# Gated linear attention: one product of 128 columns for two chunks' scores, and all low parts of the input projection's weights on VectorE

## The chip, the cores and the metric

The kernel runs on one core of a Trainium2 chip. The metric is the device time of one execution in microseconds (us). The engines are named as in the profile: PE (TensorE, matrix products), DVE (VectorE), ACT (ScalarE), POOL (GpSimd) and SP (SyncE, which issues most DMAs). Each engine has its own row of instructions, in the order in which the program issued them; an instruction waits on semaphores until what it reads is there.

## The reference, cut to what matters

One layer of a decoder for 512 prompt tokens and 8 x 4 sample tokens (544 in all), all in float32:

```python
proj = rmsnorm(x) @ w_in                 # 2048 -> 6160 columns: GLA q, k, v, gate, low-rank gate; attention q, k, v
S_t = diag(a_t) S_{t-1} + k_t^T v_t      # gated linear attention (GLA), 4 heads, key width 128, value width 256
o_t = q_t S_t
# dilated attention, 8 heads of 128: windows (128,1), (512,4), (2048,16), combined by their log-sum-exp;
# for the prompt within its 512 tokens, for the sample against a cache of 2048 rows
x = x + concat(gla_part, att_part) @ w_out
y = x + square(relu(rmsnorm(x) @ w_up)) @ w_down
```

What matters here are the scores of GLA within a chunk of 128 tokens, `A[t,s] = sum_k q[t,k] k[s,k] exp(b[t,k] - b[s,k])` for `s <= t`, with `b` the running sum of the log gates.

## The kernel before, in words

**Products in two parts.** A float32 product is made of three products of a faster format (fp32r, shown as `R32` in the code). A weight tile `raw` is rounded by ACT to its high part `wh`, and the difference `raw - wh` becomes the low part `wl`; activations are split in the same way. Each product is then wh·xh + wh·xl + wl·xh.

**The input projection** goes over 48 blocks of 128 columns (`order`), each in two slots `i` (one for each half of the 2048 rows), so that slots 0 to 95 are the projection and from slot 96 on comes w_out. Each slot has two quarters `q` of 128x512 weights. For a half slot PE does 16 products of 128x272 with `wh`, then the background work due, then 8 with `wl` (`slot_main`, L1023). `load_to` keeps three raw tiles ahead; `prep_to` calls `split_q` (L233) for the next quarter, which emits the ACT cast (`wh`) and the subtraction (`wl`), with three `wh` and three `wl` buffers. The subtraction is on POOL for slots 4 to 95 (`POOL_M` = 15: all quarters; 180 tiles in all), on DVE for the others (64 tiles). The later stages, w_up and w_down, have code of their own, in which DVE makes all low parts.

**Background work** is put between these products by `bg` (L288). It runs two lists of generators: `sgens`, the sample's attention (its step is four DVE operations on a tile `kv` of 128x640 from the cache), put in as long as the planner's clock for DVE is behind that for PE, and `gens`: the prompt's attention by heads (`att_prompt`, L437), the four GLA heads (`gla`, L685), and a norm (`att_norm`). The planner's clocks come from `Engine.cost` (L98), a price for each instruction. These prices decide where background work is put, and so the order of every row. All engine calls go through one helper, so that nearly all instructions carry its line, L95.

**An attention head** runs: scores on PE, exponent shift and maximum (custom DVE operations with the tile `st`), exp on ACT, a reciprocal on DVE, the scaling by it on ACT (out `b`, in `b,st`), transposes on PE (in `cst,b`, the identity is in `cst`), and products with v.

**A GLA head** makes the scores by levels `[64, 32, 16, 8, 4, 2, 1]`: at level w the chunk of 128 tokens is cut into blocks of 2w; queries of each block's second half (`u=1`) meet keys of its first half (`u=0`). `lev_a` (L738) takes differences of `b` against the block's middle (two DVE operations of 128x256: one for each `u`) and the exp on ACT; `lev_b` (L748) multiplies with q and k (two of 128x256) into one tile E; `lev_c` (L755) makes four products of 128x64 (one for each of the four chunks, E as the stationary operand, its `u=1` columns moving) and one COPY_PREDICATED of 128x256 into `AT` under a mask `msk`. Levels go in pairs: a step on DVE is `lev_a` of one pair, the copies of the pair before, and `lev_b`.

Of the kernel before, what the change touches and what calls it, by code (L numbers as in the profile page):

```python
# [9 lines left out]
AF = mybir.ActivationFunctionType  # L10
# [24 lines left out]
SG_C = 60  # L35
NG_A = 1
NG_G = 2
POOL_M = 15
TH_G = 2000
TH_S = 1000  # L40
LAG = 10000
# [9 lines left out]
S_FIX = 27  # L51
NUB = 4
UD = 2
POOL_SUB = 96
LEVELS = [64, 32, 16, 8, 4, 2, 1]

GQ, GK, GV, GG, GLR, AQ, AK, AV = 0, 512, 1024, 2048, 3072, 3088, 4112, 5136
# [23 lines left out]
class Engine:  # L81
# [16 lines left out]
    def cost(self, name, a, k):  # L98
        n = width(a[1] if name == "tensor_reduce" else a[0])
        if self.key == "P":  # L100
            if name == "transpose":
                return 109
            if a[1].dtype == R32:
                return 116
            return 1.68 * n if n >= 128 else 426
        if self.key == "S":
            return 100 + 0.83 * n
        if self.key == "G":
            return 120 + 2.25 * n
        if name == "tensor_copy" or name == "memset":  # L110
            return 60 + 0.7 * n
        if name == "reciprocal":
            return 60 + 6.3 * n
        return 65 + 1.07 * n + (65 if k.get("accum_out") is not None else 0)
# [8 lines left out]
def _body(ctx, nc, tc, A):  # L123
# [22 lines left out]
    def alloc(dt=F32):  # L146
        cnt[0] += 1
        n = f"b{cnt[0]}"
        for free, p, tag, bufs in tiers:
            if free[0]:  # L150
                free[0] -= 1
                t = p.tile([128, NTOK], dt, name=n, tag=tag, bufs=bufs)
                home[id(t)] = (t, free)
                return t
        raise SystemExit(f"no slots at {slot[0]} {unit_no}")
# [75 lines left out]
        spl[key] = clk[eng.key]  # L231

    def split_q(i, q):  # L233
        split_w((i, q), raws[i][:, 4 * q:4 * q + 4, :], G if 4 <= i < POOL_SUB and POOL_M >> (i % 2 * 2 + q) & 1 else V)

    def load_to(n):
        while loaded[0] < n:
# [447 lines left out]
    def gla(h):  # L685
# [49 lines left out]
        S.activation(xs[:, :128], xs[:, :128], AF.Exp)  # L735
        E = {}

        def lev_a(i):  # L738
            w = LEVELS[i]
            e = E[i] = alloc()  # L740
            ev = e[:, :SEQ].rearrange("p (n u w) -> p n u w", u=2, w=w)
            bw = bb[:, :SEQ].rearrange("p (n u w) -> p n u w", u=2, w=w)
            ref = bw[:, :, 0, w - 1:w].to_broadcast([128, SEQ // (2 * w), w])
            V.tensor_sub(ev[:, :, 1, :], bw[:, :, 1, :], ref)
            V.tensor_sub(ev[:, :, 0, :], ref, bw[:, :, 0, :])
            S.activation(e[:, :SEQ], e[:, :SEQ], AF.Exp)

        def lev_b(i):  # L748
            w = LEVELS[i]
            ev = E[i][:, :SEQ].rearrange("p (n u w) -> p n u w", u=2, w=w)  # L750
            for u, s in ((1, q), (0, k)):
                sv = s[:, :SEQ].rearrange("p (n u w) -> p n u w", u=2, w=w)
                V.tensor_mul(ev[:, :, u, :], ev[:, :, u, :], sv[:, :, u, :])

        def lev_c(i):  # L755
            b = balloc()
            w = LEVELS[i] if i < 7 else 1
            for c in range(4):
                cs = slice(c * 128, (c + 1) * 128)
                if i < 7:  # L760
                    P.matmul(b[:, c * 64:(c + 1) * 64], E[i][:, cs],
                             E[i][:, cs].rearrange("p (n u w) -> p n u w", u=2, w=w)[:, :, 1, :], start=True, stop=True)
                else:
                    P.matmul(b[:, cs], k[:, cs], q[:, cs], start=True, stop=True)
            if i < 7:
                n = 64 // w
                V.copy_predicated(AT.rearrange("p c (n u w) -> p c n u w", u=2, w=w)[:, :, :, 1, :],
                                  msk[:, i, :].rearrange("p (n u w) -> p n u w", u=2, w=w)[:, None, :, 1, :]
                                  .to_broadcast([128, 4, n, w]),
                                  b[:, :256].rearrange("p (c n w) -> p c n w", c=4, w=w))  # L770
                rel(E.pop(i))
            else:
                V.copy_predicated(AT, msk[:, i:i + 1, :].to_broadcast([128, 4, 128]),
                                  b.rearrange("p (c t) -> p c t", c=4))
            brel(b)
# [82 lines left out]
                     start=b < 4, stop=b >= 4)  # L858
        for j in range(2):
            P.transpose(b2[:32, j * 128:(j + 1) * 128], vv[j][:, SEQ:], ident)  # L860
        os_ = [alloc(), alloc()]
        tm = xs[:, 384:]
        av = b0[:, :128].rearrange("p (d b i) -> p d b i", d=4, i=4)
# [38 lines left out]
        for j in range(2):  # L902
            while len(bfree) < 1:
                yield "wait"
            b0 = balloc()
            for c in range(4):
                cs = slice(c * 128, (c + 1) * 128)
                P.matmul(b0[:, cs], vtok[:, c, j * 128:(j + 1) * 128], AT[:, c, :], start=True, stop=c == 0)
                if c:
                    P.matmul(b0[:, cs], ST[:, c, j * 128:(j + 1) * 128], qe[:, cs], start=False, stop=True)  # L910
            S.activation(os_[j][:, :SEQ], b0, AF.Copy)
            brel(b0)
            yield
        rel(qe)
        turn[0] += 1
        sq = [alloc(), alloc()]
        for j in range(2):
# [161 lines left out]
    def drain(cond, lst):  # L1079
        n = 0  # L1080
        while not cond():
            slot[0] += 1
            begin()
            clk["P"] = max(clk["P"], clk["V"], clk["S"])
            bg(2)
            n += 1
            assert n < 1000
        if DEBUG:
            print("drained", n)
# [716 lines left out]
def shape_consts():  # L1806
    f = np.float32
    cst = np.zeros((128, 546), f)
    cst[:, :128] = np.eye(128)
    s = np.arange(128)  # L1810
    cst[:, 128:256] = (s[:, None] <= s[None, :]) / 16.0
    t = np.arange(32)
    cst[:32, 256:288] = ((t[:, None] // 4 == t[None, :] // 4) & (t[:, None] <= t[None, :])) / 16.0
    bm = (np.arange(8)[:, None] == t[None, :] // 4)
    cst[:, 288:544] = bm.reshape(1, 256)
    for g in range(2):
        cst[:, 544 + g] = [SLOPES[4 * g + p // 32] for p in range(128)]
    msk = np.zeros((128, 8, 128), f)
    a, b = s[:, None], s[None, :]
    for i, w in enumerate(LEVELS):  # L1820
        msk[:, i] = (a // (2 * w) == b // (2 * w)) & (a % (2 * w) < w) & (b % (2 * w) >= w)
    msk[:, 7] = np.eye(128)

    def mult(d):
        return ((d >= 0) & (d <= 128)).astype(f) + ((d >= 0) & (d % 4 == 0) & (d <= 512)) + \
            ((d >= 0) & (d % 16 == 0) & (d <= 2048))
    d = np.arange(128)[:, None] + 384 - np.arange(512)[None, :]
    c = mult(d).astype(f)
    dc = np.stack([np.where(c > 0, -d, -1e30), np.log(np.maximum(c, 1))]).astype(f)
    i = np.arange(128) % 4  # L1830
    dist = sample_dist(i)
    c = mult(dist).astype(f)
    dcs = np.stack([np.where(c > 0, -dist, -1e30), np.log(np.maximum(c, 1))]).astype(f)
    return cst, msk, dc, dcs
# [83 lines left out]
```

## Time and profile before

| | before |
|---|---|
| median of 3 runs | 2343.21 us (2341.41 to 2343.31) |
| the profiled execution, device time | 2339.07 us |
| its span in the trace | 2337.3 us |
| mean granted PE clock | 0.996 |
| PE busy | 2289.7 us (98%) |
| DVE busy | 1993.4 us (85%) |
| ACT busy | 1114.4 us (48%) |
| POOL busy | 418.7 us (18%) |

The projection with its background work lies from about 100 to 840 us of the span; the steps of w_out, w_up and w_down follow. A row of the timeline gives the start and the length in us, the engine, the code line, the operation, its output tile and inputs, shapes, and the number of instructions run together; in square brackets stands how long the engine was idle before, and what released it. A row of the groups gives the busy time in us, the mean ns of one, and the idle time before. A row of the windows gives, for a stretch of the span, its length, the busy us of PE, PE's weight loads, DVE, ACT and POOL (with the number of instructions), the granted PE clock (1.00 is full), the DMA share and GB/s.

### The profile page before, as it was taken

To read this page: it belongs to the slowest core of one execution; us is meant where nothing else is said; L and a number is where in the kernel's file an instruction comes from. 1 tells how busy PE (TensorE), PEld (TensorE's weight loads), DVE (VectorE), ACT (ScalarE), POOL (GpSimd) and SP (SyncE) were. 2 spreads that over 40 slices of the span, in tenths; PEclk is the share of its full clock that TensorE was granted. 3 is DMA by queue.
4 is the path that set the end of the run, shared out by engine and by line. 5 is a ranking of instruction groups with operands and counts; after the bars stand their busy time and mean duration, and the time that the engine had idled before them with its cause. 6 is when DMAs were issued, how large, how long until landed. Compare 5 with 4: busy or idle time off the path is not lost.

```text
span 2337.3 us, 47617 instructions
## 1 busy us (share of the span) xinstructions
PE 2289.7 (98%) x18064; PEld 2262.0 (97%) x18064; DVE 1993.4 (85%) x4096; ACT 1114.4 (48%) x2097; POOL 418.7 (18%) x377
## 2 busy tenths in 40 slices
PE   8999999999999999899999999999999999999997
PEld 8999999999999998899999999998999999999997
DVE  6998987898887988888888888887788888888995
ACT  5333333333344235566666666665544444444465
POOL 3544553333444553000000000000000000000000
PEclk9999999999999999999999999999999999999999
DMA  6776865554725975355665556656754654664564
GB/s 239 253 265 246 291 224 206 175 175 154 248 79 166 332 243 200 113 184 195 197 208 183 185 192 208 195 185 249 272 174 161 228 200 153 223 211 156 170 215 151
DMA packets 168193, 473.46 MB, mean 203 GB/s; under 512 B 20091, under 2 KB 29307, under 8 KB 167964
## 3 DMA queue, kind: packets, MB, share of 16 engines
q1 hardware_dynamic: 157340, 439.67, 55.5%
q0 software_dynamic: 9472, 29.63, 3.9%
q8 instruction: 142, 2.33, 0.4%
q10 hardware_dynamic: 1152, 1.11, 0.1%
q14 instruction: 87, 0.71, 0.1%
HBM read 393.07 MB, written 77.27 MB: 201 GB/s over the span
## 4 chain that ended last, share of the span: by engine, by line
PE 85%; DVE 9%; issue 2%; ACT 2%; DMA 1%; SPq 0%; POOL 0%; DVEq 0%; ACTq 0%; POOLq 0%
PE bank L95 85%; DVE b L95 7%; ACT b L95 1%; DVE wl L95 1%; DMA b<-hs 0%; DVE wlP L95 0%; DVE AT L95 0%; ACT wh L95 0%; DMA kv<-kcg 0%; DVE kv L95 0%; DMA b<-vs 0%; DMA b<-xT 0%; DMA b<-wglr 0%; POOL b L95 0%; ACT L932 0%
## 5 line engine op out<-in xcount | busy, mean ns | idle before, releaser
L95 PE MATMUL bank<-b,whP 128*128 128x272 f32 x6720 | 984.5, 289 | 12.7 <-DVE b L95 4.0
L95 PEld LDWEIGHTS bank<-b,whP 128*128 128x128 f32 x6720 | 897.3, 189 | 17.0 <-ACT whP L95 5.7
L95 PE MATMUL bank<-b,wlP 128*128 128x272 f32 x3360 | 558.4, 288 | 1.1 <-DVE wlP L95 1.1
L95 PE MATMUL bank<-b,wh 128*128 128x272 f32 x3904 | 532.1, 289 | 6.1 <-ACT wh L95 5.9
L95 PEld LDWEIGHTS bank<-b,wh 128*128 128x128 f32 x3904 | 505.9, 189 | 8.5 <-ACT wh L95 8.3
L95 PEld LDWEIGHTS bank<-b,wlP 128*128 128x128 f32 x3360 | 474.4, 189 | 2.3 <-DVE wlP L95 2.3
L95 ACT ACTIVATE b<-b 128x544 fp32r<-128x544 f32 (+7 forms) x485 | 274.4, 571 | 246.6 <-DVE b L95 213.9
L95 ACT ACTIVATE whP<-b 128x512 fp32r<-128x512 f32 x480 | 300.8, 627 | 180.8 <-PE bank L95 127.9
L95 DVE TENSOR_TENSOR wlP<-b,whP 128x512 fp32r<-128x512 f32 x480 | 329.6, 688 | 29.8 <-PE bank L95 23.9
L95 POOL TENSOR_TENSOR wl<-raw,wh 128x512 fp32r<-128x512 f32 x180 | 271.0, 1511 | 384.0 <-ACT wh L95 313.0
L95 DVE TENSOR_TENSOR b<-b,b 128x272 f32<-128x272 f32 (+8 forms) x531 | 286.6, 555 | 50.5 <-ACT b L95 44.5
L95 POOL TENSOR_TENSOR b<-b,b 128x544 f32<-128x544 f32 (+2 forms) x41 | 58.3, 1425 | 1465.9 <-ACT b L95 1465.3
L95 PE MATMUL bank<-b,wl 128*128 128x272 f32 x1952 | 297.7, 295 | 0.0
L95 PEld LDWEIGHTS bank<-b,wl 128*128 128x128 f32 x1952 | 262.0, 189 | 5.9 <-issue 3.9
L95 ACT ACTIVATE wh<-raw 128x512 fp32r<-128x512 f32 x244 | 150.5, 623 | 182.0 <-PE bank L95 162.0
L95 ACT ACTIVATE b<-bank 128x272 f32<-128x272 f32 (+5 forms) x243 | 96.8, 409 | 280.2 <-PE bank L95 262.2
L95 DVE TENSOR_TENSOR b<-b,bank 128x272 f32<-128x272 f32 x388 | 167.4, 434 | 62.6 <-PE bank L95 62.2
L95 DVE TENSOR_TENSOR wlP<-mraw,whP 128x512 fp32r<-128x512 f32 x206 | 142.2, 690 | 41.0 <-ACT whP L95 40.6
L95 ACT ACTIVATE whP<-mraw 128x512 fp32r<-128x512 f32 x206 | 127.7, 626 | 89.2 <-PE bank L95 83.6
L95 DVE SCALAR_TENSOR_TENSOR kv<-kv,b 128x320 f32<-128x320 f32 x256 | 160.7, 687 | 1.6 <-DMA kv<-vcg 1.6
L95 PE MATMUL bank<-b,b 128*128 128x272 f32 (+5 forms) x968 | 143.7, 305 | 6.3 <-ACT b L95 6.3
L95 PEld LDWEIGHTS bank<-b,b 128*128 128x128 f32 (+2 forms) x968 | 119.8, 181 | 12.2 <-ACT b L95 6.4
(89 smaller groups left out, 1799.5 us busy)
## 6 DMA issues: line engine op xcount, KB each, us to landing
hs<-b SPq DMA_DIRECT2D x196, 272.0 KB, 6.0
b<-hs SPq DMA_DIRECT2D x196, 272.0 KB, 5.1
raw<-win SPq DMA_DIRECT2D x90, 512.0 KB, 4.8
mraw<-wdn SPq DMA_DIRECT2D x82, 512.0 KB, 3.9
kv<-kcg SPq DMA_DIRECT2D x64, 640.0 KB, 5.0
kv<-vcg SPq DMA_DIRECT2D x64, 640.0 KB, 4.9
mraw<-wup SPq DMA_DIRECT2D x74, 512.0 KB, 4.3
raw<-wdn SPq DMA_DIRECT2D x62, 512.0 KB, 3.8
```

The source lines that it names most:

```text
L95: return f(*a, **k)
```

## The change

**Scores.** For each level and each pair of chunks (2c, 2c+1) there is one product of 128x128: the even chunk's E is stationary, the odd chunk's E moves. To make that give both chunks' scores, the `u=1` part of E (the query side) is written with the two chunks of a pair exchanged: what stands in the even chunk's second halves belongs to the odd chunk. The odd chunk's scores come out transposed. So the mask is made symmetric, the operations on the `u=1` part in `lev_a` and `lev_b` and the COPY_PREDICATED are each split in two (`z` = 0, 1), and at the end of a head two PE transposes and one ACT copy put the odd chunks' scores into a new tile `ts`, which the output products use.

**Low parts.** All 180 tiles that POOL made are made by DVE. In the planner a product of 272 fp32r columns costs 135 instead of 116, and an empty slot at the end of the stage adds 100 to PE's clock.

```diff
-POOL_M = 15
-POOL_SUB = 96
...
             if a[1].dtype == R32:
-                return 116
+                return 135
...
     def split_q(i, q):
-        split_w((i, q), raws[i][:, 4 * q:4 * q + 4, :], G if 4 <= i < POOL_SUB and POOL_M >> (i % 2 * 2 + q) & 1 else V)
+        split_w((i, q), raws[i][:, 4 * q:4 * q + 4, :], V)
...
+        def chunks(t, w):
+            return t[:, :SEQ].rearrange("p (c z n u w) -> p z c n u w", c=2, z=2, u=2, w=w)
...
-            V.tensor_sub(ev[:, :, 1, :], bw[:, :, 1, :], ref)
             V.tensor_sub(ev[:, :, 0, :], ref, bw[:, :, 0, :])
+            ec, bc = chunks(e, w), chunks(bb, w)
+            for z in range(2):
+                V.tensor_sub(ec[:, z, :, :, 1, :], bc[:, 1 - z, :, :, 1, :],
+                             bc[:, 1 - z, :, :, 0, w - 1:w].to_broadcast([128, 2, 64 // w, w]))
...
-            for u, s in ((1, q), (0, k)):
-                sv = s[:, :SEQ].rearrange("p (n u w) -> p n u w", u=2, w=w)
-                V.tensor_mul(ev[:, :, u, :], ev[:, :, u, :], sv[:, :, u, :])
+            kv_ = k[:, :SEQ].rearrange("p (n u w) -> p n u w", u=2, w=w)
+            V.tensor_mul(ev[:, :, 0, :], ev[:, :, 0, :], kv_[:, :, 0, :])
+            ec, qc = chunks(E[i], w), chunks(q, w)
+            for z in range(2):
+                V.tensor_mul(ec[:, z, :, :, 1, :], ec[:, z, :, :, 1, :], qc[:, 1 - z, :, :, 1, :])
...
-            for c in range(4):
-                cs = slice(c * 128, (c + 1) * 128)
-                if i < 7:
-                    P.matmul(b[:, c * 64:(c + 1) * 64], E[i][:, cs],
-                             E[i][:, cs].rearrange("p (n u w) -> p n u w", u=2, w=w)[:, :, 1, :], start=True, stop=True)
...
+                for c in range(2):
+                    P.matmul(b[:, c * 128:c * 128 + 128], E[i][:, 256 * c:256 * c + 128],
+                             E[i][:, 256 * c + 128:256 * c + 256], start=True, stop=True)
...
+                for z in range(2):
+                    V.copy_predicated(av[:, z, :, :, 1 - z, :], mv[:, None, :, 1 - z, :].to_broadcast([128, 2, n, w]),
+                                      bv_[:, :, :, 1 - z, :])
...
+        for z in range(2):
+            P.transpose(b0[:, 128 + z * 128:256 + z * 128], AT[:, 2 * z + 1, :], ident)
+        ts = alloc()
+        S.activation(ts[:, :256], b0[:, 128:384], AF.Copy)
...
-                P.matmul(b0[:, cs], vtok[:, c, j * 128:(j + 1) * 128], AT[:, c, :], start=True, stop=c == 0)
+                P.matmul(b0[:, cs], vtok[:, c, j * 128:(j + 1) * 128],
+                         ts[:, (c // 2) * 128:(c // 2) * 128 + 128] if c % 2 else AT[:, c, :], start=True, stop=c == 0)
...
-            clk["P"] = max(clk["P"], clk["V"], clk["S"])
+            clk["P"] = max(clk["P"], clk["V"], clk["S"]) + 100
...
-        msk[:, i] = (a // (2 * w) == b // (2 * w)) & (a % (2 * w) < w) & (b % (2 * w) >= w)
+        msk[:, i] = (a // (2 * w) == b // (2 * w)) & ((a % (2 * w) < w) != (b % (2 * w) < w))
```

**In the rows.** From slot 96 on every engine's row is as before. Ahead of it DVE's row has 208 more instructions, POOL's 180 fewer, ACT's 4 more (the copies to `ts`), SP's as many; PE's row loses 112 products of 128x64 in 28 rows of four and gets 56 of 128x128 and 8 transposes. Tile names carry running numbers; `wl14_0` is the low part of slot 14, quarter 0.

First place: DVE's row in an attention head of the prompt, from the maximum of one group of scores (ISA rows with `st_85`) to the reciprocals of its sums (slot 14 of the projection). The four rows on `kv11` are a step of the sample's attention. Before:

```order
L95 ISA b114_1154,st_85<-bank4_70,b107_945 128x512
L95 ISA st_85 128x1
L95 TENSOR_SCALAR st_85<-st_85 128x1
L95 SCALAR_TENSOR_TENSOR b104_790<-kv11_1087,b104_790 128x320
L95 SCALAR_TENSOR_TENSOR b105_793<-kv11_1087,b104_790,b105_793 128x320
L95 SCALAR_TENSOR_TENSOR b104_790<-kv11_1087,b104_790 128x320
L95 SCALAR_TENSOR_TENSOR b105_793<-kv11_1087,b104_790,b105_793 128x320
L95 RECIPROCAL st_85<-st_85 128x1 x2
```

The same place now, where the low part of slot 14 stands ahead of the step on `kv`:

```order
L93 ISA b114_1148,st_85<-bank4_70,b107_939 128x512
L93 ISA st_85 128x1
L93 TENSOR_SCALAR st_85<-st_85 128x1
L93 TENSOR_TENSOR wl14_0_1163<-raw14_1059,wh14_0_1162 128x512
L93 SCALAR_TENSOR_TENSOR b104_818<-kv10_1081,b104_818 128x320
L93 SCALAR_TENSOR_TENSOR b105_821<-kv10_1081,b104_818,b105_821 128x320
L93 SCALAR_TENSOR_TENSOR b104_818<-kv10_1081,b104_818 128x320
L93 SCALAR_TENSOR_TENSOR b105_821<-kv10_1081,b104_818,b105_821 128x320
L93 RECIPROCAL st_85<-st_85 128x1 x2
L93 TENSOR_TENSOR wl14_1_1206<-raw14_1059,wh14_1_1205 128x512
```

The subtraction (TENSOR_TENSOR on `wl`) has come into the row between the maximum and the reciprocals, ahead of the four reads of `kv`; another follows the reciprocals.

Second place: DVE's row at one step of levels in the fourth GLA head (slot 90; `bank5`, `bank6` hold the scores of the pair of levels before). Before:

```order
L95 TENSOR_TENSOR b294_7720<-b280_7064 128x64x4 x2
L95 TENSOR_TENSOR b295_7724<-b280_7064 128x128x2 x2
L95 COPY_PREDICATED AT_79<-msk_83,bank5_71 128x16x16
L95 COPY_PREDICATED AT_79<-msk_83,bank6_72 128x32x8
L95 TENSOR_TENSOR b294_7720<-b294_7720,b270_6690 128x64x4
L95 TENSOR_TENSOR b294_7720<-b294_7720,b273_6894 128x64x4
L95 TENSOR_TENSOR b295_7724<-b295_7724,b270_6690 128x128x2
L95 TENSOR_TENSOR b295_7724<-b295_7724,b273_6894 128x128x2
```

And now:

```order
L93 TENSOR_TENSOR b298_7943<-b283_7073 128x64x4
L93 TENSOR_TENSOR b298_7943<-b283_7073 128x2x16x4 x2
L93 TENSOR_TENSOR b299_7948<-b283_7073 128x128x2
L93 TENSOR_TENSOR b299_7948<-b283_7073 128x2x32x2 x2
L93 TENSOR_TENSOR wl90_1_7962<-raw90_7842,wh90_1_7961 128x512
L93 COPY_PREDICATED AT_79<-msk_83,bank5_71 128x2x4x16 x2
L93 COPY_PREDICATED AT_79<-msk_83,bank6_72 128x2x8x8 x2
L93 TENSOR_TENSOR b298_7943<-b298_7943,b276_6894 128x64x4
L93 TENSOR_TENSOR b298_7943<-b298_7943,b272_6685 128x2x16x4 x2
L93 TENSOR_TENSOR b299_7948<-b299_7948,b276_6894 128x128x2
L93 TENSOR_TENSOR b299_7948<-b299_7948,b272_6685 128x2x32x2 x2
```

Ten DVE instructions have become sixteen, and a low part stands between `lev_a` and the copies.

More of the change, by code (lines that the diff above doesn't have):

```diff
@@ L757, in lev_c @@
             w = LEVELS[i] if i < 7 else 1
-            for c in range(4):
-                cs = slice(c * 128, (c + 1) * 128)
-                if i < 7:
-                    P.matmul(b[:, c * 64:(c + 1) * 64], E[i][:, cs],
-                             E[i][:, cs].rearrange("p (n u w) -> p n u w", u=2, w=w)[:, :, 1, :], start=True, stop=True)
-                else:
-                    P.matmul(b[:, cs], k[:, cs], q[:, cs], start=True, stop=True)
             if i < 7:
                 n = 64 // w
[L767 to L770, printed above, removed]
+                for c in range(2):
+                    P.matmul(b[:, c * 128:c * 128 + 128], E[i][:, 256 * c:256 * c + 128],
+                             E[i][:, 256 * c + 128:256 * c + 256], start=True, stop=True)
+                av = AT.rearrange("p (c z) (n u w) -> p z c n u w", z=2, u=2, w=w)
+                mv = msk[:, i, :].rearrange("p (n u w) -> p n u w", u=2, w=w)
+                bv_ = b[:, :256].rearrange("p (c n u w) -> p c n u w", c=2, u=2, w=w)
+                for z in range(2):
+                    V.copy_predicated(av[:, z, :, :, 1 - z, :], mv[:, None, :, 1 - z, :].to_broadcast([128, 2, n, w]),
+                                      bv_[:, :, :, 1 - z, :])
                 rel(E.pop(i))
             else:
+                for c in range(4):
+                    cs = slice(c * 128, (c + 1) * 128)
+                    P.matmul(b[:, cs], k[:, cs], q[:, cs], start=True, stop=True)
                 V.copy_predicated(AT, msk[:, i:i + 1, :].to_broadcast([128, 4, 128]),
@@ L913, in gla @@
             yield
-        rel(qe)
+        rel(qe, ts)
         turn[0] += 1
```

## The prediction

> **What bounds the kernel now.** First the page's busy times and its chain of waits (the work that ended last, followed back):
>
> ```profile
> PE 2289.7 (98%) x18064; PEld 2262.0 (97%) x18064; DVE 1993.4 (85%) x4096; ACT 1114.4 (48%) x2097; POOL 418.7 (18%) x377
> PE 85%; DVE 9%; issue 2%; ACT 2%; DMA 1%; SPq 0%; POOL 0%; DVEq 0%; ACTq 0%; POOLq 0%
> ```
>
> PE bounds the kernel; DVE is the only other engine with a share in the chain. So the change is worth what it takes off PE's row, less what it makes PE wait for DVE. Then the windows, with the busy time of PE, weight loads, DVE, ACT and POOL:
>
> ```profile
> 100.00:725.00 625.00, 615.84 (x4852) 598.42 (x4852) 536.46 (x1360) 225.06 (x478) 269.51 (x179) 1.00 0.58 202
> 1000.00:1100.00 100.00, 100.00 (x801) 100.00 (x800) 87.51 (x158) 63.63 (x122) 0.00 (x0) 1.00 0.63 201
> ```
>
> In the stretch that the change touches, 100 to 725 us, PE is idle for 625.00 − 615.84 = 9.2 us and DVE is 536.46/625 = 86% busy. In the other stretch POOL does nothing, DVE makes every low part at 88%, and PE never waits. So a loaded DVE is no bound by itself; it matters in which order its work stands.
>
> Who makes the low parts, and the operations beside them, by the groups (100 to 725 us for the kv rows, which the sample's attention reads, the whole span for the others), and the durations (least, median, most) of the kv operations:
>
> ```profile
> L95 POOL TENSOR_TENSOR wl<-raw,wh 128x512 fp32r<-128x512 f32 x180 | 271.0, 1511 | 384.0 <-ACT wh L95 313.0
> L95 DVE TENSOR_TENSOR wl<-raw,wh 128x512 fp32r<-128x512 f32 x64 | 46.4, 747 | 12.3 <-ACT wh L95 9.9 <-PE bank L95 2.3
> L95 DVE SCALAR_TENSOR_TENSOR kv<-kv,b 128x320 f32<-128x320 f32 x256 | 160.7, 687 | 1.6 <-DMA kv<-vcg 1.6
> L95 DVE SCALAR_TENSOR_TENSOR b<-kv,b,b 128x320 f32<-128x320 f32 x103 | 80.5, 781 | 0.0
> L95 DVE SCALAR_TENSOR_TENSOR kv<-kv,b x256: 466/482/1589, 186.2 to 644.9; 128x320 f32<-128x320 f32 x128
> L95 DVE SCALAR_TENSOR_TENSOR b<-kv,b,b x103: 532/542/1650, 100.7 to 451.6; 128x320 f32<-128x320 f32 x103
> ```
>
> The kv means lie far above their medians, and the timeline says why:
>
> ```profile
> 101.17 0.54 DVE L95 SCALAR_TENSOR_TENSOR b<-kv,b 128x320 f32<-128x320 f32 x1
> 101.19 1.65 POOL L95 TENSOR_TENSOR wl<-raw,wh 128x512 fp32r<-128x512 f32 x1 [1.21 <-ACT wh L95]
> 101.63 1.56 DVE L95 SCALAR_TENSOR_TENSOR b<-kv,b,b 128x320 f32<-128x320 f32 x1
> ```
>
> A DVE operation with two inputs in SBUF that meets a POOL subtraction takes 1.56 instead of 0.54 us. POOL's help is paid back in DVE time.
>
> **The change part by part.** All sums are against the profiled execution, 2339.07 us (span 2337.3, 1.8 around it), which lies 4.1 us below the median of 2343.21; so the forecast adds 4.1 to its own sum.
>
> *DVE's load.* Added: 162 of the 180 subtractions fall into this stretch's slots; at 0.62 (back to back, as ACT's cast of the same tile) to 0.747 us (the mean) they are 100 to 121 us. Removed: the blocking, 256 × (0.687 − 0.482) = 52 us and 103 × (0.781 − 0.542) = 25 us from the rows above, about 22 us in the other group of 103 kv reads, which alternates with this one, and (estimate) 10 to 20 us in GLA's two-input operations: 109 to 119. DVE's load stays as it was within some 15 us, at 86 to 89%, so no throughput bound. What changes is when things stand in its row.
>
> *T1, PE's work.* For the scores, two pairs of levels' products and the row behind each (background products stand as records run together, and the next row's start ends them):
>
> ```profile
> 416.26 1.90 PE L95 MATMUL bank<-b 128*128 128x64 f32 x16
> 417.96 1.24 PE L95 MATMUL bank<-b,wl 128*128 128x272 f32 x8
> 496.50 1.11 PE L95 MATMUL bank<-b,b 128*128 128x128 f32 x8
> 497.44 0.60 PE L95 MATMUL bank<-cst,b 128*128 128x128 f32 x4
> ```
>
> Sixteen records for eight products of 64 columns take 417.96 − 416.26 = 1.70 us, and eight for four products of 128 columns 497.44 − 496.50 = 0.94: a product of 64 columns costs as much as one of 128. There are 28 levels (7 in 4 heads), in 14 pairs: 14 × (1.70 − 0.94) = −10.6 us. Back come 8 transposes, at about 0.1 each +0.8. T1 = **−9.8**, all of it on PE's row, hence on the path (bounds: −10.6 if the transposes hide in a wait, −8 if records of a pair in two rows cost more).
>
> *T2, stalls that POOL makes.* Two waits and the clock behind the longer one:
>
> ```profile
> 85.55 0.78 PE L95 MATMUL bank<-cst,b 128*128 128x128 f32 x4 [1.02 <-DVE b L95]
> 317.16 0.79 PE L95 MATMUL bank<-cst,b 128*128 128x128 f32 x4 [1.80 <-DVE b L95]
> 318.00:320.00 2.00, 2.00 (x12) 1.95 (x11) 0.24 (x1) 0.68 (x2) 0.00 (x0) 0.65 0.89 291
> 320.00:322.00 2.00, 2.00 (x11) 2.00 (x10) 2.00 (x3) 0.74 (x2) 1.46 (x1) 0.50 0.99 343
> ```
>
> Both stand behind blocked DVE operations. The one at 317 costs 1.80 and, with the clock granted at 0.65 and 0.50 for two windows of 2 us, another 2 × 0.35 + 2 × 0.5 = 1.7. They go with the lock: T2 = −1.0 − 1.8 − 1.7 = **−4.5** (0 if the low part that comes into the row at this place takes as long as the blocking).
>
> *T3, the attention heads.* One head's walk before (DVE: maxima, reciprocals; ACT: casts `wh`, scaling; PE: the transposes that need the scaled scores):
>
> ```profile
> 144.81 0.62 ACT L95 ACTIVATE wh<-raw 128x512 fp32r<-128x512 f32 x1
> 147.43 0.28 DVE L95 CUSTOM_DVE_ANT_0 b<-bank,b 128x128 f32<-128x128 f32 x1
> 148.97 0.61 ACT L95 ACTIVATE wh<-raw 128x512 fp32r<-128x512 f32 x1
> 151.21 0.21 DVE L95 RECIPROCAL st<-st 128x1 f32<-128x1 f32 x2
> 153.63 0.62 ACT L95 ACTIVATE wh<-raw 128x512 fp32r<-128x512 f32 x1
> 154.64 0.21 DVE L95 RECIPROCAL st<-st 128x1 f32<-128x1 f32 x2
> 154.83 1.23 ACT L95 ACTIVATE b<-b,st 128x384 f32<-128x384 f32 x2 [0.58 <-DVE st L95]
> 155.73 2.17 PE L95 MATMUL bank<-b,wh 128*128 128x272 f32 x16
> 157.74 0.93 PE L95 MATMUL bank<-cst,b 128*128 128x128 f32 x7
> ```
>
> Now a low part stands in DVE's row ahead of each step on kv, and it can't start before ACT's cast, which stands in ACT's row behind the exp of what DVE has just shifted. Behind the waiting subtraction are queued the kv reads, and behind these the reciprocals. The walk: the first subtraction waits for the cast that ends at 145.4, takes 0.62, and the four reads are no longer blocked (−1.0): the maxima start 0.46 late. The cast after the exp then ends at 150.05, the subtraction at 150.67, the reads (4 × 0.46) at 152.5: the first reciprocals 1.3 late. Once more round: exp and cast end at 155.55, the subtraction at 156.17, the reads at 158.0, the second reciprocals 154.64 + 3.4. The scaling then ends at about 159.3, where PE wants it at 157.74: a stall of 1.5 us that wasn't there. Eight heads would make 12; two have shorter steps on kv behind them, and one has a group less: T3 = **+9** (0 where the slack of 1.7 us between scaling and transposes holds, as it did before; +16 where each head also loses its first group's slack).
>
> *T4, the levels of GLA.* A step as it is now, and the wait of the level products in the groups:
>
> ```profile
> 485.76 1.42 DVE L95 TENSOR_TENSOR b<-b 128x256 f32<-128x256 f32 x4
> 486.54 1.31 ACT L95 ACTIVATE b<-b 128x512 f32<-128x512 f32 x2 [4.04 <-DVE b L95]
> 487.10 0.99 DVE L95 COPY_PREDICATED AT<-msk,bank 128x256 f32<-128x256 uint8 x2
> 487.75 0.62 ACT L95 ACTIVATE wh<-raw 128x512 fp32r<-128x512 f32 x1
> 487.98 2.52 DVE L95 TENSOR_TENSOR b<-b,b 128x256 f32<-128x256 f32 x4
> 490.42 0.75 DVE L95 TENSOR_TENSOR b<-b 128x256 f32<-128x256 f32 x2
> L95 PE MATMUL bank<-b 128*128 128x64 f32 x224 | 27.7, 274 | 5.4 <-DVE b L95 5.3
> ```
>
> A step takes DVE 490.42 − 485.76 = 4.66 us, of which about 1.1 is blocking (2.52 against 1.42 for the four single-input operations of the same size), so 3.5 without POOL. Now: differences 1.47 (two operations have become three; the halves carry about 0.03 more each, by bounds 0 to 0.2), then the subtraction, which waits for both exps (1.31 from the first tile's end) and the cast behind them (0.62): 1.25 idle; 0.62 for itself; four copies of half the size 1.24; products 1.47: **6.05 us**. PE's half slot is 24 products at (157.74 − 155.73)/16 = 0.126, 3.0 us, and 0.94 for a pair of levels, 3.9. Where steps follow in every half slot, PE waits up to 2.1 us. Nine of the twelve intervals within the four heads are such; the hand walk, with the slack at each head's start, gives 14 us of waits, against the 5.4 above: T4 = **+9** (−5, if the waits go with the lock; +16, if all nine cost 2.1 and the head's end as much again).
>
> The split operations otherwise cost DVE time in its slack, the copies to `ts` four short ACT operations (ACT is at 36% here), the transposes are in T1. SP's row is the same, so no load moves.
>
> *T5, the clock.* After the 1.80 us wait the granted clock fell to 0.50. I expect two of the new waits to be so long, each at 1.7 us: **+3.5** (0 to +8). [...]
>
> Sum: −9.8 − 4.5 + 9 + 9 + 3.5 = +7.2, so 2346.3 by its own time and **2350** against the median.
>
> What speaks for such waits is in before itself, in w_out, where DVE already makes the low parts:
>
> ```profile
> 913.23 0.61 ACT L95 ACTIVATE wh<-raw 128x512 fp32r<-128x512 f32 x1
> 913.88 1.50 DVE L95 TENSOR_TENSOR wl<-raw,wh 128x512 fp32r<-128x512 f32 x1 [1.89 <-ACT wh L95]
> 913.90 0.77 PE L95 MATMUL bank<-b,wh 128*128 128x272 f32 x4 [0.70 <-ACT wh L95]
> ```
>
> DVE stood 1.89 us for ACT's cast, with its other work queued behind, and PE lost 0.70.
>
> **The rivals.**
>
> *B, faster: the lock was the cause of the waits.* If DVE's row, rid of blocked operations, keeps ahead of PE, T3 and T5 are 0 and T4 is 0: −9.8 − 4.5 = −14.3, **2329** (2322, if the GLA waits go too, to 2337). For it: the blocking removed is worth as much as the subtractions, and at 1000 us DVE makes all low parts with PE at 100%. Against: in the heads DVE hangs on ACT, which it does not at 1000 us. It decides if the waits in T3's walk stay below 1.7 us. [...]
>
> *D, about the same: only GLA waits.* T3 = 0, T5 one drop: −9.8 − 4.5 + 9 + 1.7 = −3.6, **2340** (2336 to 2344). For it: 1.7 us of slack in the attention heads.
>
> *C, clearly slower: DVE becomes the bound.* If half of the blocking comes back otherwise (55 of 109 us), DVE stands at (536 + 65)/625 = 96%, and its waits for ACT no longer fit: some 25 us over, less 14.3, with clock drops 3.5: +14 to +20, **2360**. Against: the window at 1000 us.
>
> **How the numbers follow.** My forecast 0.43 (its own range 2344 to 2362), B 0.29, D 0.18, C 0.10. A run tells 0.2%, 4.7 us, from no change: faster is below 2338.5, slower above 2347.9. Faster: all of B and a fifth of D, 0.32. Slower: C and 0.83 of mine, 0.46. The same: 0.22. The range leaves out B's lower end and C's upper: 2328 to 2364.
>
> **What would show it right or wrong.** Right: new DVE waits of PE in front of `bank<-cst,b` transposes in most attention heads, over 1 us each; the level products (128x128) waiting 10 to 16 us for DVE; kv means at their medians; DVE idle for ACT's `wh` in front of `wl`. Wrong: PE idle below 8 us between 100 and 725 (then B), or DVE at 95% there (then C).

## The result: slower by 22 us, at three times the forecast loss

The changed kernel takes 2364.34 us (median of 4 runs, 2363.31 to 2366.47) against 2342.31 us before (2339.32 to 2343.31); the ratio is 1.0095, with a 95% interval of 1.0081 to 1.0109. The direction was the forecast's, the size was not: +22 us where +7 were expected, just outside the range's upper end of 2364.0.

The page of the changed kernel, its busy times and its chain:

```profile
PE 2289.8 (97%) x17960; PEld 2257.2 (96%) x17960; DVE 1967.9 (83%) x4360; ACT 1114.9 (47%) x2101; POOL 148.3 (6%) x197
PE 76%; DVE 13%; DMA 4%; issue 4%; ACT 3%; POOL 0%; SPq 0%; DVEq 0%; ACTq 0%; POOLq 0%
```

The span is 2361.5 us. DVE is busy for 25.5 us less than before, although its row has 264 more instructions (4360 against 4096: 180 low parts and 84 from the split operations, not 208 in all as said under the change): the blocking by POOL is gone. Yet PE's share of the chain fell from 85 to 76%, and DVE's, the DMAs' and ACT's rose. The window of 100 to 725 us, and the groups that the prediction spoke of (kv and `wl` rows for 100 to 725 us, the PE rows for 100 to 780):

```profile
100.00:725.00 625.00, 597.18 (x4649) 575.96 (x4650) 495.42 (x1577) 215.06 (x467) 22.54 (x15) 0.99 0.58 203
L93 DVE TENSOR_TENSOR wl<-raw,wh 128x512 fp32r<-128x512 f32 x157 | 112.4, 720 | 83.7 <-ACT wh L93 75.0 <-PE bank L93 8.5
L93 DVE SCALAR_TENSOR_TENSOR kv<-kv,b 128x320 f32<-128x320 f32 x256 | 110.5, 485 | 0.0
L93 PE MATMUL bank<-cst,b 128*128 128x128 f32 x212 | 32.6, 278 | 12.1 <-ACT b L93 10.8 <-DVE b L93 0.7
L93 PE MATMUL bank<-b 128*128 128x128 f32 x112 | 17.7, 291 | 9.3 <-DVE b L93 9.1
L93 PE MATMUL bank<-b,ones 128*128 128x272 f32 x20 | 6.7, 458 | 5.3 <-DVE b L93 5.3
L93 PE MATMUL bank<-b,wh 128*128 128x272 f32 x2729 | 373.4, 289 | 5.4 <-ACT wh L93 5.4
```

The PE rows before, for the transposes and for `wh`, from 100 to 780 us:

```profile
L95 PE MATMUL bank<-cst,b 128*128 128x128 f32 x205 | 29.8, 274 | 1.9 <-DVE b L95 1.8
L95 PE MATMUL bank<-b,wh 128*128 128x272 f32 x2842 | 387.0, 289 | 1.4 <-ACT wh L95 1.2
```

PE is idle for 27.8 us there instead of 9.2. DVE is busy for 495 us instead of 536, and stands idle for 83.7 us in front of the low parts, 75.0 of them for ACT's cast. The kv reads are at 485 ns instead of 687. So DVE has lost no time to work; it stands still in its row. PE's waits lie in front of four things: the attention heads' transposes, the level products, the norms' products with `ones`, and the weights `wh` themselves.

Where the 22 us (24.2 between the two spans) build up is read from the start of the same quarter of the projection in both traces, that is, PE's first product with that quarter's `wh`. Before (quarters 0, 12, 96, 160 and 184 of the stretch, of which the attention heads take 12 to 96, three GLA heads 96 to 160, the fourth and the norms the rest):

```profile
46.11 2.17 PE L95 MATMUL bank<-b,wh 128*128 128x272 f32 x16
82.35 2.17 PE L95 MATMUL bank<-b,wh 128*128 128x272 f32 x16
400.52 2.17 PE L95 MATMUL bank<-b,wh 128*128 128x272 f32 x16
658.18 2.05 PE L95 MATMUL bank<-b,wh 128*128 128x272 f32 x15
751.40 2.17 PE L95 MATMUL bank<-b,wh 128*128 128x272 f32 x16
```

The same five quarters now:

```profile
48.09 0.29 PE L93 MATMUL bank<-b,wh 128*128 128x272 f32 x1
84.91 2.18 PE L93 MATMUL bank<-b,wh 128*128 128x272 f32 x16
415.37 2.17 PE L93 MATMUL bank<-b,wh 128*128 128x272 f32 x16
671.95 2.17 PE L93 MATMUL bank<-b,wh 128*128 128x272 f32 x16
772.87 2.16 PE L93 MATMUL bank<-b,wh 128*128 128x272 f32 x16
```

The lag is 2.0, 2.6, 14.9, 13.8 and 21.5 us. So the attention heads cost 12.3 us, the first three GLA heads give back 1.1 with PE's shorter products in them, and the fourth GLA head with the norms costs 7.7. In this last stretch the lag first falls to 4.8 (quarter 166), since the fourth head's level products begin there and not at quarter 160 as before, and then climbs to 21.5. Behind slot 96, where all rows are as before, 2.7 us come in small steps up to the end of the span.

The walk in the changed kernel, in the same attention head as in the prediction (low parts and reciprocals on DVE, scaling on ACT, transposes on PE):

```profile
150.86 0.69 DVE L93 TENSOR_TENSOR wl<-raw,wh 128x512 fp32r<-128x512 f32 x1 [0.82 <-ACT wh L93]
155.52 1.14 DVE L93 TENSOR_TENSOR wl<-raw,wh 128x512 fp32r<-128x512 f32 x1 [1.19 <-ACT wh L93]
161.50 0.69 DVE L93 TENSOR_TENSOR wl<-raw,wh 128x512 fp32r<-128x512 f32 x1 [1.41 <-ACT wh L93]
163.96 0.21 DVE L93 RECIPROCAL st<-st 128x1 f32<-128x1 f32 x2
164.21 1.23 ACT L93 ACTIVATE b<-b,st 128x384 f32<-128x384 f32 x2 [2.74 <-DVE st L93]
164.88 1.27 PE L93 MATMUL bank<-cst,b 128*128 128x128 f32 x7 [1.71 <-ACT b L93]
```

Three low parts in a row wait for ACT, the kv reads and the reciprocals come behind them, and PE waits 1.71 us (1.5 was forecast). The seven transposes then take 1.27 us where they took 0.93.

At the end of the stage, DVE's and PE's rows around the last norm:

```profile
746.07 0.78 DVE L93 SCALAR_TENSOR_TENSOR b<-b,nw,b 128x544 f32<-128x544 f32 x1
747.57 0.72 DVE L93 TENSOR_TENSOR b<-b,b 128x544 fp32r<-128x544 f32 x1 [0.72 <-ACT b L93]
749.51 0.71 DVE L93 TENSOR_TENSOR b<-b,b 128x544 f32<-128x544 f32 x1
750.28 2.18 PE L93 MATMUL bank<-b,ones 128*128 128x272 f32 x4 [3.34 <-DVE b L93]
```

The attention norm multiplies, waits 0.72 us for ACT's rounding, subtracts, and so on for eight heads; the sum of squares at 749.51 that PE wants stands behind this, and PE waits 3.34 us. Before, the same products waited for nothing:

```profile
717.59 1.08 PE L95 MATMUL bank<-b,ones 128*128 128x272 f32 x4
```

And the clock: in windows of 10 us from 40 to 780 us, the shares of the clock not granted sum up to 1.7 us before and 6.8 now, most of it in these three, behind waits of 2.53, 2.43 and 3.34 us:

```profile
340.00:350.00 10.00, 9.50 (x67) 9.05 (x66) 6.71 (x16) 3.54 (x10) 0.00 (x0) 0.86 0.30 113
420.00:430.00 10.00, 7.57 (x49) 7.35 (x48) 8.79 (x29) 2.94 (x6) 0.00 (x0) 0.83 0.43 157
750.00:760.00 10.00, 9.72 (x54) 9.26 (x55) 8.04 (x16) 4.60 (x9) 0.00 (x0) 0.71 0.67 248
```

### The profile page after: what moved, and what is told of

It reads as the page before. It is cut to its first block, busy times and chain, and to the rows that moved or that the text cites. A ratio compares the mean times of both kernels' runs of the same rounds, so it can differ in the third digit from the quotient of the medians.

```text
span 2361.5 us, 47485 instructions
## 1 busy us (share of the span) xinstructions
PE 2289.8 (97%) x17960; PEld 2257.2 (96%) x17960; DVE 1967.9 (83%) x4360; ACT 1114.9 (47%) x2101; POOL 148.3 (6%) x197
## 4 chain that ended last, share of the span: by engine, by line
PE 76%; DVE 13%; DMA 4%; issue 4%; ACT 3%; POOL 0%; SPq 0%; DVEq 0%; ACTq 0%; POOLq 0%
PE bank L93 76%; DVE b L93 9%; DVE wl L93 2%; ACT b L93 2%; ACT wh L93 1%; DMA b<-vs 1%; DMA kv<-kcg 1%; DVE kv L93 1%; DMA b<-hs 1%; DMA b<-win 0%; DMA gs<-b 0%; DMA b<-xT 0%; DVE wlP L93 0%; DVE st L93 0%; DVE AT L93 0%
## 5 line engine op out<-in xcount | busy, mean ns | idle before, releaser
L93 PEld LDWEIGHTS bank<-b,wh 128*128 128x128 f32 x3904 | 507.6, 189 | 13.3 <-ACT wh L93 12.6
L93 ACT ACTIVATE b<-b 128x544 fp32r<-128x544 f32 (+6 forms) x485 | 274.0, 571 | 246.2 <-DVE b L93 217.4
L93 DVE TENSOR_TENSOR b<-b,b 128x272 f32<-128x272 f32 (+8 forms) x559 | 261.4, 486 | 41.5 <-ACT b L93 38.6
L93 DVE TENSOR_TENSOR wl<-raw,wh 128x512 fp32r<-128x512 f32 x244 | 174.6, 726 | 101.6 <-ACT wh L93 89.7
L93 ACT ACTIVATE b<-bank 128x272 f32<-128x272 f32 (+4 forms) x247 | 97.8, 409 | 275.6 <-PE bank L93 246.3
L93 PEld LDWEIGHTS bank<-b,b 128*128 128x128 f32 (+2 forms) x968 | 119.9, 180 | 12.6 <-ACT b L93 6.8
L93 DVE TENSOR_TENSOR wlP<-raw,whP 128x512 fp32r<-128x512 f32 x154 | 105.5, 685 | 29.8 <-ACT whP L93 29.7
```

The lines of the kernel that those rows point to most:

```text
L93: return f(*a, **k)
```

## The experiments

Theory at the start: the low parts' place in DVE's row makes PE wait, and PE's gain of 10 us on the scores comes out whatever else is done. Rivals: DVE has too much to do; the split operations of the scores cost it; the planner's prices have moved work. Ratios are to the kernel before, run beside each.

### Which half of the change, and which stage

**The low parts alone.** Before, with

```diff
-POOL_M = 15
+POOL_M = 0
...
-                return 116
+                return 135
...
-            clk["P"] = max(clk["P"], clk["V"], clk["S"])
+            clk["P"] = max(clk["P"], clk["V"], clk["S"]) + 100
```

> The kernel before with all low parts on DVE (and the planner's 135 and +100), its scores still in products of 64 columns. Theory (the low parts in DVE's row make PE wait, the products of 128 columns save 9.8 us whatever else is done): the changed kernel's 22 us over before, plus 10, so 2374 (2368 to 2380), with the attention heads' waits before the transposes as in the changed kernel, 11 to 12 us. Rival (the scores' split DVE operations bring a good part of the waits): 2350 to 2360.

Measured: 2365.01 us, ratio 1.0099 (1.0083 to 1.0114). The waits for ACT and DVE in front of the transposes are about the changed kernel's, 11.8 us against 11.5. But the time is the changed kernel's too: over the whole the new scores bring it nothing, neither the gain of the theory nor the loss of the rival. By stages they do something: from quarter 96 to 160, the first three GLA heads, the lag grows by 7.1 us here and falls by 1.1 in the changed kernel, and in the fourth head with the norms it grows by 3.5 here and by 7.7 there.

**The scores alone.** The changed kernel with POOL for slots 4 to 95, 116 and no +100.

```diff
-        split_w((i, q), raws[i][:, 4 * q:4 * q + 4, :], V)
+        split_w((i, q), raws[i][:, 4 * q:4 * q + 4, :], G if 4 <= i < 96 else V)
```

> The changed scores alone: low parts on POOL as before, planner at 116 and without the +100. Theory: PE's work falls by 9.8 us and the level waits stay near 5.4, so 2333 (2330 to 2336), faster by 0.4%. Rival (the split DVE operations, with POOL's blocking still there, lengthen each step of levels, which PE then waits for): 2338 to 2346, no gain.

Measured: 2343.68 us, ratio 1.0011 (1.0001 to 1.0020). No gain; the theory's 2333 is out. PE's products are shorter: a pair of levels in the changed kernel and the row behind it,

```profile
431.54 1.05 PE L93 MATMUL bank<-b 128*128 128x128 f32 x8
432.35 1.25 PE L93 MATMUL bank<-b,wl 128*128 128x272 f32 x8
```

take 0.81 us instead of 1.70. So the saving is there, and something gives it back.

**POOL in one stage.** The changed kernel with `G if 4 <= i < 48 else V` (heads), and with `G if 48 <= i < 96 else V` (GLA and norms).

> The changed kernel, but POOL makes the low parts of slots 4 to 47, the stretch of the attention heads; DVE those of slots 48 to 95, the GLA heads and the norm. Theory (each stage pays for its own rows): the heads' 12 us go, the rest stays: 2352 (2348 to 2356). Rival (it is DVE's total work that is late, and the heads' delay only hands on what comes later): 2340 or 2364, that is all or nothing.

> The changed kernel, but POOL makes the low parts of slots 48 to 95, the GLA heads and the norm; DVE those of slots 4 to 47. Theory (each stage pays for its own rows): the heads' 12 us stay, and against before there is also the gain of 9.8 us: 2346 (2342 to 2352). Rival (delays of the heads are made up in the GLA stage when DVE has less there): 2335 or less.

Measured: POOL in the heads 2351.24 us, ratio 1.0036 (1.0023 to 1.0049), as the theory had it: 13 us off the changed kernel. In its trace 9 of the heads' 12.3 us go, and the rest of the 13 comes in small parts elsewhere. POOL in the GLA stage 2370.10 us, ratio 1.0120 (1.0105 to 1.0135): no better than DVE there but 6 us worse, which neither expected. PE's waits for DVE in front of the level products are 15.4 us in it, with one of 5.16 us. What of that is POOL's blocking and what the planner's price was not separated.

### What takes the scores' gain

**The planner's clocks held.** The scores alone, with the clocks set back to the old scores' cost, so that DVE's row differs from before only in the levels.

```diff
+                    clk["P"] += 637
...
+                clk["V"] -= 65
```

> The changed scores alone, low parts on POOL, with the planner's clocks for them set back to what the old scores cost it (each product of 128 columns priced 637 higher, each split pair 65 lower), so that outside the levels DVE's row is as before. Theory (the gain of 10 to 12 us on PE was lost because the planner, thinking PE's part shorter, put the fourth GLA head and the norm later): 2331 (2328 to 2335). Rival (the split operations make each step of levels too long for PE, wherever it stands): 2339 to 2345 as in the run of the scores alone.

Measured: 2345.18 us, ratio 1.0021 (1.0011 to 1.0030). My theory that the planner's placement took the gain falls. The level products now wait 12.6 us for DVE, against 5.4 before.

**PE's part alone.** The same, with DVE's operations on the levels as before, not split; the chunks are not exchanged, so this computes other scores.

```diff
-            for z in range(2):
-                V.tensor_mul(ec[:, z, :, :, 1, :], ec[:, z, :, :, 1, :], qc[:, 1 - z, :, :, 1, :])
+            V.tensor_mul(ev[:, :, 1, :], ev[:, :, 1, :], qv_[:, :, 1, :])
```

> Low parts on POOL, planner's clocks as before, products of 128 columns, but the DVE operations on the levels left as before (not split, the chunks not exchanged, so the scores are not those of the reference; what the exchange would add is left out). Theory (the split operations make the steps of levels longer than PE's half slot): the gain of 10 us on PE comes out, 2331 (2328 to 2335). Rival (the step of levels on DVE, 4.66 us, is the bound of that stretch already before, so that PE's shorter part only waits longer): 2337 to 2342, level waits on PE of 11 us or more against 5.3.

Measured: 2341.93 us, ratio 1.0007 (0.9997 to 1.0016), the rival's number. Its level products, from 100 to 780 us:

```profile
L93 PE MATMUL bank<-b 128*128 128x128 f32 x112 | 17.8, 291 | 11.1 <-DVE b L93 11.1
```

Nothing was added to DVE, PE has 10 us less to do, and it waits 5.7 us longer for DVE in front of these products and 3.4 us longer in front of `wh` and `ones` (1.7 each). Already before, a step of levels took DVE 4.66 us and PE's half slot 3.0 + 1.7 = 4.7: the two were even. PE's part shortened alone gains nothing. The split operations add some 3 us to this (2345.18 against 2341.93).

### What the planner's price does

**The price alone, on the kernel before** (135 and +100).

> The kernel before with the planner's 135 and +100 alone. Theory (the price only decides how many kv reads stand in a slot, and PE waits little there): 2341 (2337 to 2346). Rival (at 135 the planner gives DVE more than it can do beside POOL's blocking): 2350 to 2357.

Measured: 2347.90 us, ratio 1.0035 (1.0022 to 1.0048), between the two, about 8 us slower; 3.3 us of it is one wait of PE for a cast, at 712.53 us.

**The changed kernel at 116.**

> The changed kernel with the planner's price for a product of 272 fp32r columns at 116 as before (the +100 stays). Theory (with DVE's clock charged for 180 subtractions, a price of 116 leaves the background work no room in the slots; it piles up behind slot 95, where nothing covers it): 2375 to 2395, with PE waits of over 10 us just ahead of w_out. Rival (135 itself costs the 8 us that it costs the kernel before): 2354 to 2358.

Measured: 2410.57 us, ratio 1.0298 (1.0283 to 1.0313). Theory and more: the work that finds no room is done behind the slots. Windows of 10 us there:

```profile
730.00:740.00 10.00, 3.89 (x17) 3.36 (x17) 10.00 (x46) 1.72 (x3) 0.00 (x0) 0.50 0.44 129
760.00:770.00 10.00, 1.39 (x4) 0.50 (x2) 9.73 (x31) 5.56 (x8) 0.00 (x0) 0.50 0.64 239
```

DVE is busy to the last tenth, PE at 39 and 14%, and its clock at half. So 135 belongs to the low parts on DVE: without it they cost 46 us more, though it costs the kernel before 8.

**Low parts of the GLA stage on DVE, in the kernel before at 116** (`4 <= i < 48` in its rule for POOL).

> The kernel before, old scores and planner, but DVE makes the low parts of slots 48 to 95 (GLA heads and norm). Theory (in the GLA stage POOL's blocking costs as much as the subtractions, as the run with POOL in that stage shows, 6 us slower than the changed kernel): 2338 (2333 to 2343). Rival (each step of levels waits for ACT's cast, the prediction's T4): 2348 to 2354.

Measured: 2376.38 us, ratio 1.0155 (1.0138 to 1.0172). Neither: it is the same pile behind the slots, with one wait of 9.47 us:

```profile
764.02 2.18 PE L95 MATMUL bank<-b,ones 128*128 128x272 f32 x4 [9.47 <-DVE b L95]
```

So this run says nothing on POOL's blocking against DVE's subtractions, for which it was made.

### The place in DVE's row

**Cast and subtraction behind the background work.**

```diff
-        prep_to(uidx[i] + 3)
...
-            if q == 0:
-                prep_to(uidx[i] + 4)
+            prep_to(uidx[i] + 3 + q)
```

> The changed kernel with each quarter's cast and subtraction written behind the half slot's background work instead of ahead of it, so that in DVE's row the low part stands behind the kv reads and the reciprocals. DVE has as much to do. Theory (the heads wait because a low part that waits for ACT stands ahead of the reciprocals): the 11 us of waits in front of the heads' transposes go, 2352 (2348 to 2357). Rival (DVE's load): they stay, 2362 to 2367.

Measured: 2378.94 us, ratio 1.0167 (1.0152 to 1.0182), worse than both theories. In the heads the subtraction still stood ahead of the next step on kv, so the order that I meant to change was kept; in the levels the cast now stood behind the exps in ACT's row, and PE waited 26.0 us for `wh` (100 to 780 us; 5.4 in the changed kernel). The edit did not do what it was for; the next one moves the subtraction alone.

**The subtraction alone, behind the step on kv** (slots 10 to 93). The cast stays, the planner's clocks and all other rows are kept: in the traces PE, ACT and POOL have the changed kernel's instructions in its order, and DVE has the same 4360 in another.

```diff
         S.activation(whm[key], r, AF.Copy)
-        V.tensor_sub(wlm[key], r, whm[key].bitcast(F32))
+        lows.append((key, r))
...
         while clk["V"] + 1000 < clk["P"] + TH_S and step(sgens):
             pass
+        low_out()
```

> The changed kernel; the casts stay where they are, but each subtraction of slots 10 to 93 is written behind the step on kv that it stood ahead of. The planner's clocks and so all other rows are the changed kernel's; DVE has as much to do. (The run that moved cast and subtraction together behind the background work left the subtraction ahead of the next step on kv, so it did not try this.) Theory (in the heads DVE stands still for ACT's exp and cast, with the kv reads and the reciprocals queued behind): the kv reads, 1.85 us, now run while ACT works; the waits ahead of the heads' transposes fall from 11 us to 3 or less, 2353 (2349 to 2357). Rival (DVE's load: 0.6 us for each low part is too much between two half slots): the waits stay at 9 us or more, 2361 to 2366.

Measured: 2345.98 us, ratio 1.0022 (1.0012 to 1.0031): 18 us off the changed kernel (16 if each is taken against the kernel before beside it, 2342.31 and 2340.21) by an edit that adds and removes nothing, and 7 us below the forecast. DVE's low parts and the heads' transposes (100 to 780 us):

```profile
L93 DVE TENSOR_TENSOR wl<-raw,wh 128x512 fp32r<-128x512 f32 x175 | 122.7, 705 | 30.6 <-ACT wh L93 29.0 <-PE bank L93 1.2
L93 PE MATMUL bank<-cst,b 128*128 128x128 f32 x205 | 30.0, 275 | 3.8 <-ACT b L93 2.2 <-DVE b L93 1.3
```

DVE stands still for 30.6 instead of 83.7 us, and the transposes wait 3.8 instead of 12.1. The rival, DVE's load, is out: the load is the same.

**The subtraction behind all of the half slot's background work** (again DVE's order alone), so that in ACT's row the cast stands ahead of the exps.

```diff
             if q or BG2:
                 bg(nbg)
+            low_out()
```

> The changed kernel with each subtraction of slots 10 to 93 written behind all of the half slot's background work, its cast still ahead of that work, so that in ACT's row the cast stands ahead of the exps and DVE has not to wait for it, in the heads and in the GLA levels. All else as the changed kernel. Theory (what is left of the GLA waits after the kv step's run, 9.3 us of level products and 4.3 us of casts, is again the subtraction that waits behind exp and cast): level waits of 5 us or less, 2337 (2332 to 2341). Rival (DVE's step is too long even without standing still, 4.8 us against PE's 3.9): level waits stay at 8 us or more, 2343 to 2347.

Measured: 2331.83 us, ratio 0.9963 (0.9949 to 0.9976): faster than before, and 5 us better than forecast.

```profile
L93 DVE TENSOR_TENSOR wl<-raw,wh 128x512 fp32r<-128x512 f32 x181 | 124.1, 692 | 6.0 <-ACT wh L93 3.7 <-PE bank L93 1.5 <-issue 0.3
L93 PE MATMUL bank<-b 128*128 128x128 f32 x112 | 16.5, 282 | 2.7 <-DVE b L93 2.4
```

DVE now stands 6.0 us in front of its low parts, the level products wait 2.7 (9.5 in the run before this one), and the wait for casts (4.3) is gone. The changed kernel's loss by the low parts' place is 2364.34 − 2331.83 = 32.5 us, or 31.0 if each is taken against the kernel before beside it (2342.31 and 2340.77).

**The same with the old scores.**

> The same place for the subtractions, but with the old scores (products of 64 columns, four copies of before), planner at 135 and +100. Theory (where DVE's step bounds the levels, PE's saving does nothing, so old and new scores are alike): within 4 us of the run with the new scores. Rival (once DVE does not stand still, the 10 us of PE come out): 7 us or more slower than that run.

Measured: 2335.81 us, ratio 0.9977 (0.9968 to 0.9987). With DVE no longer standing still, the new scores are worth 4.0 us, just at the bound of the theory and short of the rival's 7. At quarter 160, behind three GLA heads, they are worth 6.5 (the lag against before is −12.9 and −6.4 us), but from there on the fourth head's gain and more is lost again: the norms' products wait 5.7 us with the new scores, 1.5 with the old.

**The last norm two heads at a time.** In the changed kernel, and in the one with the subtractions behind the background work.

```diff
-            V.scalar_tensor_tensor(AO[h], AO[h], nw[:, 48 + h:49 + h], r, op0=OP.mult, op1=OP.mult)
-            a, b = alloc(R32), alloc(R32)
-            put_x(a, b, AO[h])
+            for j in (h, h + 1):
+                V.scalar_tensor_tensor(AO[j], AO[j], nw[:, 48 + j:49 + j], r, op0=OP.mult, op1=OP.mult)
+            ab = [(alloc(R32), alloc(R32)) for j in range(2)]
+            for j in range(2):
+                S.activation(ab[j][0], AO[h + j], AF.Copy)
+            for j in range(2):
+                V.tensor_sub(ab[j][1], AO[h + j], ab[j][0].bitcast(F32))
```

> The changed kernel with the attention norm's last steps written two heads at a time: both multiplications, both casts, both subtractions, instead of one head after the other, so that DVE does not stand 0.72 us for ACT in each. Nothing else. Theory (of the 7.7 us that the changed kernel loses from the fourth GLA head to slot 90, the 3.3 us wait of the last norm's products stands behind this ping-pong, and the clock drops behind it): 2358 (2355 to 2361). Rival (the wait comes from the levels and moves elsewhere): 2362 to 2366.

> Both edits: subtractions behind the background work, the norm two heads at a time. Theory (the two are in different places and add up): 2332 (2327 to 2336), faster than the kernel before by 0.2 to 0.5%. Rival (DVE's longer steps in the levels keep what the row order gave back): 2338 to 2343, no faster than before.

Measured: the changed kernel with it 2357.87 us, ratio 1.0070 (1.0056 to 1.0084), 6.5 us off, as forecast. Both edits 2327.30 us, ratio 0.9939 (0.9927 to 0.9952): all but 2 us of the two gains (32.5 and 6.5) add up, and this is 13.5 us faster than the kernel before (2340.77 beside it) and 37 than the changed one.

## Why the prediction was wrong

The direction and most of the mechanism were right; the sum was too small. Between the two profiled executions +7.2 us were forecast and 24.2 came, 17.0 more. By stages, 7.8 of it lie in the attention heads (T2 and T3: +4.5 forecast, 12.3 measured) and 7.9 in the fourth GLA head and the norms (−0.2 forecast, a quarter of T1 and T4; 7.7 measured). 2.6 lie ahead of the heads and 2.7 behind slot 96, where the sum had nothing; the first three GLA heads are 0.5 better, and T5's 3.5 lies inside these stages. So two steps failed: the heads' terms were sized too small, and the end of the stage had no term.

- **What bounds it, and DVE's load: right.** The load did not rise. kv's blocking fell by 160.7 − 110.5 = 50 us (52 forecast), DVE has slack, and only the order in its row matters, as two edits that move the subtraction alone show (−18 and −32.5 us). The kv reads took 687 ns on average beside POOL's subtractions and 485 without; rival B, which had the blocking as the cause of the waits, did not come.
- **T1, "−9.8, all of it on PE's row, hence on the path": failed as a gain of its own.** The size on PE was right, 0.89 us a pair (0.76 forecast). But the levels' half slots were as long on DVE (4.66 us) as on PE (4.7), and without any other edit PE's saving brought nothing (2341.93); beside the low parts it brought 0.7 (2365.01 against 2364.34). The time being on PE's row, 98% busy on average, is not the same as being on the path in that stretch. The numbers for seeing it stood in the prediction itself, under T1 and T4. In the sum this did little harm, since T4 counted its waits against the shortened half slot of 3.9 us.
- **T2, −4.5: mostly wrong.** The wait at 85 us went and the one at 317 fell from 1.80 to 0.69 (at 327.08), but the heads' new waits stand in their place (1.46 us at 100.51, 2.53 at 338.58), and so does the clock drop.
- **T3, the heads, +9: mechanism right, size too small.** The walk was right to 0.2 us in the head for which it was made. The waits in the heads are 11.5 us against 2.8; the transposes behind them take 0.34 us longer in each of eight heads, 2.7, which the sum left out; together 11.4 of the measured 12.3, where T2 and T3 had +4.5.
- **T4, the levels, +9: right.** The level products and casts wait 9.3 + 5.4 = 14.7 us against 6.8. T1 and T4 together were forecast as −0.8 for four heads; the first three gave −1.1. The four operations that T4 calls single-input, 1.42 us, are differences of two operands from one tile, 414 ns each before and 417 now (128x256, 100 to 780 us), so they took as long beside POOL's subtractions as without. The products of that size took 719 ns before and 434 now, 4 × 0.285 = 1.14 us for a step's four: the 1.1 us of blocking holds.
- **T5, the clock, +3.5: 5.1 measured.** A size.
- **What the sum did not hold.** The fourth GLA head and the norms, and the first 2.0 us. The planner's prices stood in the diff and had no term, and they decide where the fourth head stands. Its level products start at quarter 160 before and at 166 now, while the attention norm, whose turns between DVE and ACT lie ahead of PE's products, ends at 181 in both. The 135 is not what puts them late: alone on the kernel before, it starts them at 153. With the low parts on DVE as well it is 161, with the new scores, which the planner prices lower, 166, and without the 135 (the changed kernel at 116) 179. Giving the norm two heads at a time takes 6.5 us of the loss. What makes the first 2.0 us, ahead of quarter 0, was not tried; over the kernels tried this lag is between −0.4 and 3.1 us.
- **Rival C** gave nearly the right number (2360) by the wrong cause: DVE is 79% busy in that stretch, not 96.

Open: why POOL in the GLA stage alone is 6 us slower than DVE there, how the 8 us of the price on the kernel before divide, and the 2.0 us at the start and 2.7 at the end.

## What to carry to other kernels

An instruction that waits for another engine is paid by everything queued behind it: issue its producer early in the producer's row and itself late in its own; here DVE stood still for 83.7 us in front of its low parts, and their place alone was worth 31 to 32 us of 2364, with the same instructions. Before counting time taken off the busiest engine as a gain, look at the stretch it is taken from: if a second engine's step there is as long (here 4.66 us on DVE against 4.7 on PE), the first one will only wait. And a price in a planner is part of the change: it decides what is left over at the end of a stage, where nothing covers it.

## What the runs showed of the hardware that was not expected

The granted clock fell behind a wait of PE of 1.80 us (at 317 before, to 0.50 from 320 to 322 us) and behind one of 2.43 us (at 424 in the changed kernel). The length of a wait alone does not decide in these runs: in the changed kernel with the norm two heads at a time the same products waited 2.44 us (at 425.52), and the clock stayed at 1.00. The products and a stretch of the clock, first in the changed kernel, then in that run:

```profile
423.98 3.47 PE L93 MATMUL bank<-b,wh 128*128 128x272 f32 x16 [2.43 <-ACT wh L93]
427.25 1.45 PE L93 MATMUL bank<-b 128*128 128x128 f32 x8
424.65:428.06 3.41, 3.41 (x17) 3.41 (x17) 3.06 (x7) 0.32 (x1) 0.00 (x0) 0.50 0.40 150
425.52 2.27 PE L93 MATMUL bank<-b,wh 128*128 128x272 f32 x16 [2.44 <-ACT wh L93]
427.62 1.05 PE L93 MATMUL bank<-b 128*128 128x128 f32 x8
423.95:427.36 3.41, 1.84 (x14) 1.84 (x15) 2.77 (x8) 2.51 (x6) 0.00 (x0) 1.00 0.00 0
```

Up to the next row the sixteen products with `wh` took 427.25 − 423.98 = 3.27 us in the changed kernel and 427.62 − 425.52 = 2.10 in that run. What separates the two waits these rows do not show.
